# Up and down projections of a gated feed-forward block as seven block products in place of eight

## The chip, the cores and the metric

The kernel runs on one core of a Trainium2 chip. The metric is the time of one execution on the device in microseconds; a profile of one execution gives the span from its first to its last instruction. Engines are named TensorE (PE, its weight loads PEld), VectorE (DVE), ScalarE (ACT), GpSimd (POOL) and SyncE (SP, which issues DMAs).

## The reference

One layer of an encoder on 512 tokens of 2048 features, all in float32:

```python
h = rmsnorm(x, norm_mix[l])
proj = h @ w_in[l]                        # 2048 x 8704
...                                       # window attention A, neighbourhood attention B
merged = (jax.nn.sigmoid(ga) * (out_a @ w_branch_a[l])
          + jax.nn.sigmoid(gb) * (out_b @ w_branch_b[l]))
x = x + merged @ w_out[l]
h2 = rmsnorm(x, norm_ffn[l])
u = h2 @ w_up[l]                          # 2048 x 11264
u = up[:, :-2] * cw[0] + up[:, 1:-1] * cw[1] + up[:, 2:] * cw[2] + conv_b[l]   # up is u, padded
gate, val = jnp.split(u, 2, axis=-1)
x = x + (jax.nn.silu(gate) * val) @ w_down[l]   # 5632 x 2048
```

The change concerns the last five lines: the product with `w_up`, a convolution of width 3 over the tokens, the gate, and the product with `w_down`.

## The kernel before, in words

Activations lie with features on the 128 partitions and the 512 tokens along the free axis, 16 tiles for 2048 features. Every float32 operand of a product is split into two exact parts, `hi` (rounded to the type that TensorE multiplies at full rate) and `lo` (the rest), and a product is three matmuls: hi with hi, hi with lo, lo with hi (`run_step`, lines 146 to 175). All products are *steps*: 512 output columns of a weight matrix against 16, 8 or 4 activation tiles, in blocks of 1024 weight elements a partition (two activation tiles of 512 columns). A step accumulates in four of the eight PSUM banks, while the other four are being read out.

Weights come in by `stage` (line 118): SP issues one DMA of 512 KB into one of three buffers `raw`, ScalarE makes `hi` (line 135), VectorE `lo` (line 136), each in two buffers. One block is staged while the block before is multiplied: 24 matmuls of 512 columns.

The stages run in this order: the input projection with both attentions (the heads' softmax work is put into a queue and done behind the next step's matmuls; GpSimd takes small powers, line 192), gates and branches, the output projection with the residual into `x2` (line 563), and the gated block. That last part has eleven chunks of 512 features: `up(c)` makes gate and value for chunk c (two steps of eight blocks), each tile is scaled, convolved and gated by `conv` and its callers (lines 573 to 596), and the result is split into `acts`. `down(c - 1)` follows: four steps of two blocks whose sums are added to `x2` (line 610); the last chunk's results go out from there. The activations between up and down never leave SBUF.

The program is recorded in the order of the loops, and a scheduler puts each engine's instructions into an order of their own. SP's DMAs keep the order of the program among themselves.

Of the kernel before, what the change touches and what calls it, by code (L numbers as in the profile page):

```python
# [18 lines left out]
P = 128  # L19
D = 2048  # L20
S = 512
# [6 lines left out]
SMALLS = (("gffn", 16), ("gqb", 1), ("gkb", 1), ("sink", 8), ("gqa", 128), ("gka", 128),  # L28
          ("cos", 256), ("sin", 256), ("mask_a", 384), ("mask_b", 112),
          ("conv_w", 264), ("conv_b", 88))  # L30
N_SLOTS, N_P, N_TR, AHEAD = 60, 8, 4, 400
ATTENTION_RATE, RATE = 1.25, 3
READY = (2, 4, 6, 9, 12, 15, 16, 16)
# [4 lines left out]
def trunk_kernel(  # L38
# [10 lines left out]
    wst = pool("wst", 3)  # L49
# [3 lines left out]
    att_ctx = ExitStack()  # L53
# [35 lines left out]
    smalls = const.tile([P, small_in.shape[1]], F32, tag="smalls", name="smalls")  # L89
    part, at = {}, 0  # L90
    for name, width in SMALLS:
        part[name] = smalls[:, at:at + width]
        at += width
# [6 lines left out]
    def load_smalls():  # L100
        dma(smalls, small_in)
# [4 lines left out]
    steps, stream, queue = [], [], deque()  # L106

    def step(layout, w, cols, acts, evac, k0=0, nk=KD, before=None, pre=None, post=None, rate=RATE):
        """layout "f": out[col, tok], weights stationary; "t": out[tok, col], weights moving."""
        width = sum(n for _, n in cols)  # L110
        kpb = 1024 // width
        steps.append((layout, kpb, width, nk, acts, evac, before, pre, post, rate))
        for k in range(0, nk, kpb):
            stream.append((w, k0 + k, kpb, cols))

    staged = deque()

    def stage(pieces=1):
        if not stream:
            return  # L120
        w, k, kpb, cols = stream.pop(0)
        raw = wst.tile([P, 1024], F32, tag="raw", name="raw", bufs=3)
        hi = wst.tile([P, 1024], F32R, tag="hi", name="hi", bufs=2)
        lo = wst.tile([P, 1024], F32R, tag="lo", name="lo", bufs=2)
        view, at = raw.rearrange("p (a n) -> p a n", a=kpb), 0
        for c, n in cols:
            for a in range(0, kpb, kpb // pieces):
                b = a + kpb // pieces
                dma(
                    view[:, a:b, at:at + n],  # L130
                    w[(k + a) * P:(k + b) * P, c:c + n].rearrange("(a p) n -> p a n", p=P))
            at += n
        n = 1024 // pieces
        for c in range(0, 1024, n):
            nc.scalar.copy(hi[:, c:c + n], raw[:, c:c + n])  # L135
            nc.vector.tensor_tensor(  # L136
                lo[:, c:c + n], raw[:, c:c + n], hi[:, c:c + n].bitcast(F32), ALU.subtract)
        staged.append((hi.rearrange("p (a n) -> p a n", a=kpb),
                       lo.rearrange("p (a n) -> p a n", a=kpb)))
# [6 lines left out]
    def run_step(layout, kpb, width, nk, acts, evac, before, pre, post, rate):  # L146
# [4 lines left out]
        for kb in range(nk // kpb):  # L151
            if before:
                before(kb)
            hi, lo = staged.popleft()
            stage()
# [32 lines left out]
    # ---- RMSNorm over the features: the gain goes into the transposed activations, the  # L188
# [5 lines left out]
    def square_sum(name, k, src):  # L194
        """Squares summed over the 16 tiles of features."""
# [8 lines left out]
    def row_factor(name):  # L204
        """rs[tok, t], and the same along the free axis on every partition."""
# [7 lines left out]
        b = bank("tr" if "tr" in banks else "mm")  # L213
# [17 lines left out]
    def first_loads():  # L231
        load_xT(1)
        hT.append(split(xt[0], g=gmix[:, :1]))
        stage(2)
        load_xT(1)
        stage()
# [54 lines left out]
    def row_heads(cols, nh, rotate, finish, on_evac=None, then=(), **kw):  # L291
        """Heads out of 512 columns: rows normalised and transposed behind the next step."""
# [86 lines left out]
    def behind(finish=None):  # L379
        """Softmax of one head ahead of the transposes and the product with v of the last one."""  # L380
# [115 lines left out]
    post = {}  # L496

    def end_attention():
# [3 lines left out]
        post["pool"] = pool("post", 1)  # L502
# [3 lines left out]
    def extra(dt=F32):  # L506
        return post["pool"].tile([P, S], dt, tag="e", name="e", bufs=14)

    sga, sgb, merged, oa, ob = {}, {}, [None] * KD, [], []

    def gates(c0, store, base, alloc, **kw):
        def evac(m, ps):
            s = alloc()
            nc.vector.tensor_tensor(s, ps, rows["m"], ALU.mult)  # L514
            store[base + m] = s

        step("f", w_in, [(c0 + base * P, 512)], hT, evac, **kw)
# [3 lines left out]

    def evac_a(m, ps):
        s = sga[m]
        nc.scalar.activation(s, s, AF.Sigmoid)  # L524
# [165 lines left out]
```

## Time and profile before

| | us |
|---|---|
| median of 3 runs (lowest, highest) | 2634.92 (2634.89, 2636.03) |
| span of the profiled execution | 2634.1 |
| TensorE busy in it | 2623.6 |
| VectorE busy | 1258.4 |
| ScalarE busy | 840.8 |
| GpSimd busy | 34.4 |
| window of the up and down projections, 1192 to 2631 us | 1439 |

The profiled execution's own time is its span of 2634.1 us; the median of the runs is 0.8 us more. How to read the views that the prediction quotes: a group line gives source line, engine, operation, output<-inputs, shapes and count, then busy us and mean ns of one, then the idle time of the engine before it and what ended it. A line of a tile's view gives shortest/median/longest ns. A timeline line gives start and length in us, engine, line, operation, count. A line of the windows gives the stretch, its length, the busy us of PE, PEld, DVE, ACT and POOL with their counts, TensorE's granted clock, the DMA engines' busy share and GB/s. Matmuls overlap in TensorE's pipeline: what one costs is the time from its start to the next one's.

### The profile page before, as it was taken

The page shows a single profiled execution, that of the slowest core. Times are in us where ns is not written, and L with a number is a line of the kernel's source. Part 1 is how long each engine was busy: PE and PEld are TensorE (multiplying, and loading weights), DVE is VectorE, ACT ScalarE, POOL GpSimd, SP SyncE. Part 2 cuts the span into 40 slices and gives each one's busy share as a digit, 9 for nine tenths or more (in the row PEclk, how much of TensorE's full clock was granted, in tenths as well). Part 3 has the DMA queues.
Part 4 walks back from the last instruction along what each step waited for, and adds up shares of the span by engine and source line. Part 5 has one row for each costly group of instructions (what it writes and reads, how often), then busy time and mean ns, then how long its engine had stood idle before and what let it go on. Part 6 is the DMA issues. An engine that isn't in the chain of part 4 may idle for free.

```text
span 2634.1 us, 28831 instructions
## 1 busy us (share of the span) xinstructions
PE 2623.6 (100%) x11848; PEld 2182.7 (83%) x11848; DVE 1258.4 (48%) x1685; ACT 840.8 (32%) x1156; POOL 34.4 (1%) x38
## 2 busy tenths in 40 slices
PE   9999999999999999999999999999999999999999
PEld 7888888888888888888888888888888888888887
DVE  6565545542333344435453636363636363636364
ACT  5355544532222222323232323231323232323231
POOL 0100000000000000000000000000000000000000
PEclk9999999999999999999999999999999999999999
DMA  5322222333233323332323232333333333332333
GB/s 181 96 89 85 90 94 90 114 107 115 98 96 96 112 96 127 113 114 94 96 96 101 95 100 97 96 96 96 96 97 98 100 97 96 96 97 96 96 96 128
DMA packets 152115, 268.53 MB, mean 102 GB/s; under 512 B 9520, under 2 KB 35120, under 8 KB 151984
## 3 DMA queue, kind: packets, MB, share of 16 engines
q1 hardware_dynamic: 147376, 258.31, 30.7%
q10 hardware_dynamic: 4608, 8.39, 0.8%
q8 instruction: 92, 1.51, 0.2%
q14 instruction: 39, 0.32, 0.0%
HBM read 258.27 MB, written 8.39 MB: 101 GB/s over the span
## 4 chain that ended last, share of the span: by engine, by line
PE 100%; DMA 0%; DVE 0%; ACT 0%; issue 0%; SPq 0%; ACTq 0%
PE mm L74 96%; PE tr L74 2%; PE tr L430 1%; PE tr L288 0%; PE tr L337 0%; DMA s<-in_x_t 0%; PE mm L217 0%; PE tr L217 0%; PE mm L208 0%; ACT s L183 0%; DVE s L514 0%; DVE s L610 0%; PE tr L208 0%; ACT hi L135 0%; SPq L71 0%
## 5 line engine op out<-in xcount | busy, mean ns | idle before, releaser
L74 PE MATMUL mm<-s,hi 128*128 128x512 f32 x6528 | 1937.0, 389 | 0.9 <-DVE s L514 0.9
L74 PEld LDWEIGHTS mm<-s,hi 128*128 128x128 f32 x6528 | 1224.5, 188 | 253.7 <-ACT s L524 1.3
L74 PE MATMUL mm<-s,lo 128*128 128x512 f32 x3264 | 1193.7, 389 | 0.0
L136 DVE TENSOR_TENSOR lo<-raw,hi 128x1024 fp32r<-128x1024 f32 (+1 forms) x465 | 568.1, 1222 | 1161.7 <-ACT hi L135 1159.1
L135 ACT CAST hi<-raw 128x1024 fp32r<-128x1024 f32 (+1 forms) x465 | 489.1, 1052 | 1507.3 <-PE mm L74 1332.7
L74 PEld LDWEIGHTS mm<-s,lo 128*128 128x128 f32 x3264 | 612.6, 188 | 126.6
L74 PE MATMUL mm<-hi,s 128*128 128x512 f32 x896 | 285.5, 395 | 5.8 <-ACT hi L135 5.8
L74 PEld LDWEIGHTS mm<-hi,s 128*128 128x128 f32 x896 | 168.6, 189 | 39.0 <-ACT hi L135 5.8
L74 PE MATMUL mm<-lo,s 128*128 128x512 f32 x448 | 176.8, 396 | 0.0
L610 DVE TENSOR_TENSOR e<-mm,e 128x512 f32<-128x512 f32 x132 | 90.1, 689 | 23.5 <-PE mm L74 23.2
L74 PEld LDWEIGHTS mm<-lo,s 128*128 128x128 f32 x448 | 84.9, 190 | 16.5
L576 ACT ACTIVATE s<-t,smalls 128x512 f32<-128x512 f32 x88 | 71.4, 811 | 42.6 <-DVE t L575 42.6
L577 DVE SCALAR_TENSOR_TENSOR s<-t,smalls,s 128x511 f32<-128x511 f32 x88 | 65.8, 748 | 10.1 <-ACT s L576 9.7
L579 DVE SCALAR_TENSOR_TENSOR s<-t,smalls,s 128x511 f32<-128x511 f32 x88 | 65.9, 749 | 2.4
L575 DVE TENSOR_TENSOR t<-mm,row 128x512 f32<-128x512 f32 x88 | 60.4, 687 | 2.4 <-PE mm L74 2.4
L435 DVE TENSOR_TENSOR pl<-tr,ph 128x256 fp32r<-128x256 f32 (+1 forms) x64 | 30.2, 485 | 29.7 <-ACT ph L434 29.6
L589 ACT ACTIVATE t<-s 128x512 f32<-128x512 f32 x44 | 27.8, 631 | 51.0 <-DVE s L579 51.0
L409 ACT ACTIVATE p<-p,nm 128x256 f32<-128x256 f32 (+1 forms) x64 | 35.4, 555 | 23.8 <-DVE nm L402 15.9
L434 ACT CAST ph<-tr 128x256 fp32r<-128x256 f32 (+1 forms) x64 | 26.1, 421 | 47.4 <-PE tr L74 22.1
L610 DVE TENSOR_TENSOR s<-mm,s 128x512 f32<-128x512 f32 x44 | 30.4, 692 | 19.9 <-PE mm L74 19.9
L74 PE MATMUL tr<-ph,s 128*128 128x256 f32 (+1 forms) x128 | 37.7, 313 | 0.0
L180 ACT CAST s<-s 128x512 fp32r<-128x512 f32 x52 | 32.0, 619 | 17.5 <-DVE s L531 9.7
(102 smaller groups left out, 849.8 us busy)
## 6 DMA issues: line engine op xcount, KB each, us to landing
raw<-in_w_up SPq DMA_DIRECT2D x176, 512.0 KB, 3.5
raw<-in_w_in SPq DMA_DIRECT2D x103, 512.0 KB, 3.6
raw<-in_w_down SPq DMA_DIRECT2D x88, 512.0 KB, 3.6
raw<-in_w_in SPq DMA_DIRECT2D x66, 256.0 KB, 3.1
raw<-in_w_out SPq DMA_DIRECT2D x32, 512.0 KB, 3.7
raw<-in_w_branch_a SPq DMA_DIRECT2D x16, 512.0 KB, 3.6
raw<-in_w_branch_b SPq DMA_DIRECT2D x16, 512.0 KB, 3.7
s<-in_x_t SPq DMA_DIRECT2D x20, 256.0 KB, 6.1
```

What stands on the lines that cost most here:

```text
L74: nc.tensor.matmul(o, l, r, start=start, stop=stop, skip_group_check=True)
L135: nc.scalar.copy(hi[:, c:c + n], raw[:, c:c + n])
L136: nc.vector.tensor_tensor(lo[:, c:c + n], raw[:, c:c + n], hi[:, c:c + n].bitcast(F32), ALU.subtract)
L180: nc.scalar.copy(hi, src)
L409: nc.scalar.activation(pr[j][:, :n], pr[j][:, :n], AF.Exp, bias=nm[:, j:j + 1], accum_out=sm[:, j:j + 1])
L435: nc.vector.tensor_tensor(pl[:, :n], b[:, :n], ph[:, :n].bitcast(F32), ALU.subtract)
L575: nc.vector.tensor_tensor(u, ps, rows["f"], ALU.mult)
L576: nc.scalar.activation(o, u, AF.Identity, bias=cb[:, idx:idx + 1], scale=cw[:, idx, 1:2])
L577: nc.vector.scalar_tensor_tensor(o[:, 1:], u[:, :S - 1], cw[:, idx, 0:1], o[:, 1:], op0=ALU.mult, op1=ALU.add)
L579: nc.vector.scalar_tensor_tensor(o[:, :S - 1], u[:, 1:], cw[:, idx, 2:3], o[:, :S - 1], op0=ALU.mult, op1=ALU.add)
L589: nc.scalar.activation(sg, g, AF.Sigmoid)
L610: nc.vector.tensor_tensor(x2[m], ps, x2[m], ALU.add)
```

## The change

Both projections of the gated block become products of 2x2 blocks in seven multiplications (Strassen's, in Winograd's form). The blocks are: pairs of activation tiles (first and second 128 features of a pair), two halves of the output columns, and the two halves of the tokens (256 each). A *unit* (`Product`) is one pair of activation tiles and 256 columns out of each half of the output: seven weight forms of 256 columns, seven activation forms, 42 matmuls of 256 tokens.

- Weight forms: SP loads five of the seven 256-column pieces of a unit from DRAM (640 KB in three DMAs, rows of 1 KB, four units ahead). A DMA issued by GpSimd adds two further pieces onto them (three units ahead), and two additions of 256 elements on GpSimd make the remaining forms (two units ahead). ScalarE and VectorE split the forms as before, in parts of four and three forms (1024 and 768 elements), one unit ahead.
- Activation forms: `forms` makes seven forms of a pair with four subtractions or additions and seven splits of 256 elements on VectorE and seven copies on ScalarE.
- Sums: a group of units with the same columns (8 in the up projection; 8 or 7 in the down projection) accumulates seven PSUM banks; `combine` puts the four output blocks together, one ScalarE copy and seven VectorE instructions, into tiles of 1024 elements.
- The up projection runs first, 22 groups. Scaling with the row factor moves to GpSimd (line 767, 1024 elements, twice a group). The gated activations are written to DRAM (`act`, line 792) and read back in the down projection (line 835).
- The down projection runs in three parts of 8, 7 and 7 pairs. The sums of the first two parts are added by DMAs from GpSimd onto `total` in DRAM, where the residual `x2` has been put before; the last part adds them on VectorE and writes the output.
- Ahead of that, gates and branches are reordered (gate tiles are held in fewer buffers), and the staging buffers are freed after the output projection for the split weight forms.

The core of the diff:

```diff
-    def up(c):
-        ...
-        step("f", w_up, [(c * 512, 512)], h2T, evac_gate, before=before)
-        step("f", w_up, [(D_FF + c * 512, 512)], h2T, evac_val)
-    def down(c, acts, last):
-        ...
-            step("f", w_down, [(n * 512, 512)], acts, evac, k0=c * 4, nk=4)
+    def advance():
+        for phase, d in (("load", 4), ("add", 3), ("sums", 2)):
+            while at[phase] < min(at["use"] + d + 1, len(units)):
+                ...
+                    getattr(u, phase)()
+                at[phase] += 1
+        prep_to(at["use"] + 1)
+    class Product:
+        def load(self):
+            s = slice(self.c, self.c + 256)
+            self.f = ffn["f"].tile([P, 7, 256], F32, tag="f", name="f", bufs=4)
+            dma(self.f[:, 0:2], self.w[:, :, 0, s])
+            dma(self.f[:, 2:4], self.w[:, 0, :, s])
+            dma(self.f[:, 6], self.w[:, 1, 1, s])
+        def add(self):
+            tc.keep_in_program_order(nc.gpsimd.dma_start(
+                self.f[:, 2:4], self.w[:, :, 1, s], accum_op=ALU.add))
+        def sums(self):
+            nc.gpsimd.tensor_tensor(f[:, 4], f[:, 2], f[:, 6], ALU.add)
+            nc.gpsimd.tensor_tensor(f[:, 5], f[:, 4], f[:, 1], ALU.add)
+        def prep(self):
+            for tag, a, b in (("a", 0, 4), ("b", 4, 7)):
+                ...
+                nc.scalar.copy(hi, self.f[:, a:b])
+                nc.vector.tensor_tensor(lo, self.f[:, a:b], hi.bitcast(F32), ALU.subtract)
+    def forms(src):
+        nc.vector.tensor_tensor(t[:, 0], y[:, 3], y[:, 1], ALU.subtract)
+        nc.vector.tensor_tensor(t[:, 1], y[:, 0], y[:, 1], ALU.subtract)
+        nc.vector.tensor_tensor(t[:, 2], t[:, 0], y[:, 0], ALU.add)
+        nc.vector.tensor_tensor(t[:, 3], t[:, 2], y[:, 2], ALU.subtract)
+        for v in (y[:, 0], y[:, 2], t[:, 0], t[:, 1], t[:, 2], y[:, 3], t[:, 3]):
+            nc.scalar.copy(o[:, :256], v)
+            nc.vector.tensor_tensor(o[:, 256:], v, o[:, :256].bitcast(F32), ALU.subtract)
+    def products(w, c, pairs, acts, evac, before=None):
+            for i, j in enumerate(pairs):
+                u = next_unit()
+                for f, (wh, wl) in enumerate(u.parts):
+                    a = acts[j][f]
+                    for m in range(2):
+                            mm(o, wh[:, s], a[:, :256], i == m == 0, False)
+                            mm(o, wh[:, s], a[:, 256:], False, False)
+                        mm(o, wl[:, s], a[:, :256], False, i == len(pairs) - 1 and m == 1)
+                if i == len(pairs) - 1:
+                    combine(ps, evac)
+                advance()
+                run_queued(1)
+    def combine(ps, evac):
+        q1, q2, q7, q5, q6, q3, q4 = [p.rearrange("p (m n) -> p m n", m=2) for p in ps]
+        nc.scalar.copy(p1, q1)
+        nc.vector.tensor_tensor(top[:, :, left], q2, p1, ALU.add)
+        nc.vector.tensor_tensor(p1, p1, q6, ALU.subtract)
+        nc.vector.scalar_tensor_tensor(u3, q7, -1.0, p1, op0=ALU.mult, op1=ALU.subtract)
+        nc.vector.tensor_tensor(low[:, :, right], u3, q5, ALU.subtract)
+        nc.vector.tensor_tensor(p1, p1, q5, ALU.add)
+        nc.vector.tensor_tensor(top[:, :, right], q3, p1, ALU.add)
+        nc.vector.tensor_tensor(low[:, :, left], u3, q4, ALU.subtract)
+    def conv(u, idx):
+        nc.gpsimd.tensor_tensor(u, u, row, ALU.mult)
+        ...
+            def val_part():
+                v = conv(val, 44 + 2 * s)
+                nc.vector.tensor_tensor(v, gate, v, ALU.mult)
+                dma(act[s], v)
+    def down(part, pairs, nxt=()):
+                    if nxt:
+                        nc.gpsimd.dma_start(total[h][s], t, accum_op=ALU.add)
+                    else:
+                        nc.vector.tensor_tensor(t, t, old[h], ALU.add)
+                        ...
+                if s == 3 and skip <= i < skip + len(nxt):
+                    form_down(part + 1, nxt[i - skip])
+    for s in range(pairs_ff):
+        up(s)
+    down(0, range(0, 8), range(8, 15))
+    down(1, range(8, 15), range(15, 22))
+    down(2, range(15, 22))
```

The order of SP's DMAs in the middle of the up and down projections before (`raw` is a weight buffer; every row is a run of loads):

```order
L71 DMA raw<-in_w_up 128x2x512 x16
L71 DMA raw<-in_w_down 128x2x512 x8
L71 DMA raw<-in_w_up 128x2x512 x16
L71 DMA raw<-in_w_down 128x2x512 x8
L71 DMA raw<-in_w_up 128x2x512 x16
```

And SP's order around the end of one up group after (`f` are a unit's weight pieces, `act_138` the activations in DRAM, `w_14327` the tile that holds the gated values; two rows are one unit's loads, the ones behind the store are the loads of the seventh unit of the next group):

```order
L73 DMA f<-in_w_up 128x2x256 x2
L73 DMA f<-in_w_up 128x256
L73 DMA f<-in_w_up 128x2x256 x2
L73 DMA f<-in_w_up 128x256
L73 DMA act_138<-w_14327 128x1024
L73 DMA f<-in_w_up 128x2x256 x2
L73 DMA f<-in_w_up 128x256
```

A store of activations has come into the row of loads, which had nothing but loads before.

VectorE's order in an up step before (`lo` is the split of a weight block, lines 575 to 595 are the convolution and the gate):

```order
L595 TENSOR_TENSOR s<-s 128x512
L136 TENSOR_TENSOR lo<-raw,hi 128x1024
L181 TENSOR_TENSOR s<-s 128x512
L577 SCALAR_TENSOR_TENSOR s<-t,smalls,s 128x511
L579 SCALAR_TENSOR_TENSOR s<-t,smalls,s 128x511
L595 TENSOR_TENSOR s<-s 128x512
L136 TENSOR_TENSOR lo<-raw,hi 128x1024
```

VectorE's order behind the end of the same up group after (lines 631 to 635 are `combine`, line 569 the split of weight forms, `w_14226` and `w_14327` gate and value):

```order
L631 SCALAR_TENSOR_TENSOR t<-mm,t 128x512
L569 TENSOR_TENSOR wl<-f,wh 128x768
L632 TENSOR_TENSOR w_14227<-t,mm 128x2x256
L633 TENSOR_TENSOR t<-t,mm 128x512
L635 TENSOR_TENSOR w_14227<-t,mm 128x2x256
L634 TENSOR_TENSOR w_14226<-mm,t 128x2x256
```

```order
L787 TENSOR_TENSOR w_14226<-w_14226,w_14253 128x1024
L569 TENSOR_TENSOR wl<-f,wh 128x768
L569 TENSOR_TENSOR wl<-f,wh 128x1024
L791 TENSOR_TENSOR w_14327<-w_14226,w_14327 128x1024
L569 TENSOR_TENSOR wl<-f,wh 128x768
L569 TENSOR_TENSOR wl<-f,wh 128x1024
```

The splits of the weight forms now stand between the steps of `combine` and of the gate; the last product of a group (line 791), for which the store waits, stands behind the first split of the next group's sixth unit.

More of the change, by code (lines that the diff above doesn't have):

```diff
@@ L111, in step @@
         kpb = 1024 // width
-        steps.append((layout, kpb, width, nk, acts, evac, before, pre, post, rate))
+        steps.append(partial(
+            run_step, layout, kpb, width, nk, acts, evac, before, pre, post, rate))
         for k in range(0, nk, kpb):
[L114 to L139, printed above, removed]
@@ L141, in run_queued, with next_unit @@
+    def next_unit():
+        u = units[at["use"]]
+        at["use"] += 1
+        return u
     def run_queued(n):
```

296 lines of the change are left out of this document (214 added, 82 removed).

## Prediction

> **What bounds the kernel now.** I read the page's first and fourth parts, then the chain in order of time, then the busy time by windows of the span.
>
> ```profile
> span 2634.1 us, 28831 instructions
> PE 2623.6 (100%) x11848; PEld 2182.7 (83%) x11848; DVE 1258.4 (48%) x1685; ACT 840.8 (32%) x1156; POOL 34.4 (1%) x38
> PE 100%; DMA 0%; DVE 0%; ACT 0%; issue 0%; SPq 0%; ACTq 0%
> 1227.18 1403.09 PE mm L74 x6190
> 520.00:1165.00 645.00, 644.13 (x2863) 533.85 (x2862) 243.66 (x279) 183.06 (x226) 0.00 (x0) 1.00 0.34 108
> 1192.00:2631.00 1439.00, 1438.26 (x6354) 1190.83 (x6352) 705.33 (x848) 397.09 (x444) 1.93 (x1) 1.00 0.31 98
> ```
>
> TensorE is the chain from end to end, at a granted clock of 1.00. Its last piece is 6,190 matmuls of 512 columns in 1403.09 us: 226.7 ns from one to the next. The two projections of the last block (up and down) fill the window from 1192 to 2631 us: 1439 us, in which VectorE works 705 us, ScalarE 397 us, GpSimd 2 us, and the DMA engines 31% of the time at 98 GB/s. Everything but TensorE has room. So the change is worth what it takes off TensorE in these 1439 us, less what its new work makes TensorE wait.
>
> **Fewer columns.** Before: 88 x 16 x 3 matmuls for the up projection and 16 x 44 x 3 for the down, 6336 of 512 columns. After: 264 units (22 groups of 8 up, 88 units down), each with seven products x two tiles of output columns x three split terms = 42 matmuls of 256 columns: 11088. The columns fall to 7/8. The price of a 256-column matmul stands in the attention stage. These rows are TensorE's timeline at two places: start, length, what, count.
>
> ```profile
> 126.38 0.52 PE L74 MATMUL tr<-s 128*128 128x256 f32 x3
> 126.73 0.63 PE L74 MATMUL mm<-hi,s 128*128 128x512 f32 x2
> 137.34 0.52 PE L74 MATMUL tr<-s 128*128 128x256 f32 x3
> 137.70 0.40 PE L74 MATMUL mm<-lo,s 128*128 128x512 f32 x1
> L74 PEld LDWEIGHTS mm<-s,hi 128*128 128x128 f32 x6528 | 1224.5, 188 | 253.7 <-ACT s L524 1.3
> ```
>
> Three take 0.35 us and 0.36 us until the next begins: 117 to 120 ns each, 118 taken, although each has its own weight load of 188 ns. Half of 226.7 would be 113; the narrow matmul costs 4% more a column. 11088 x 0.118 = 1308 us, against 1439: **131 us off**, and 122 to 142 at 119 and 117. A unit is 42 x 0.118 = 4.96 us, a group of eight 39.65 us.
>
> **The work per unit that TensorE must not wait for.** These are groups by line and shape (count, busy us, mean ns).
>
> ```profile
> L136 DVE TENSOR_TENSOR lo<-raw,hi 128x1024 fp32r<-128x1024 f32 x463 | 566.8, 1224 | 1161.7 <-ACT hi L135 1159.1 <-PE mm L74 2.2
> L135 ACT CAST hi<-raw 128x1024 fp32r<-128x1024 f32 x463 | 487.8, 1054 | 1507.3 <-PE mm L74 1332.7 <-issue 170.9 <-DMA raw<-in_w_in 1.1
> L181 DVE TENSOR_TENSOR s<-s 128x512 fp32r<-128x512 f32 x52 | 35.6, 685 | 0.2
> L610 DVE TENSOR_TENSOR e<-mm,e 128x512 f32<-128x512 f32 x132 | 90.1, 689 | 23.5 <-PE mm L74 23.2
> L579 DVE SCALAR_TENSOR_TENSOR s<-t,smalls,s 128x511 f32<-128x511 f32 x88 | 65.9, 749 | 2.4
> L281 DVE TENSOR_TENSOR qr<-t 128x256 f32<-128x256 f32 x8 | 3.4, 420 | 0.0
> L434 ACT CAST ph<-tr 128x256 fp32r<-128x256 f32 x32 | 11.9, 371 | 40.0 <-PE tr L74 21.2 <-PE tr L430 15.6 <-DVE rq L261 3.2
> ```
>
> The seven weight forms are split as 1024 and 768 elements. VectorE: 1.22 us, and 0.96 (halfway between 685 and 1224), 2.18 us a unit. ScalarE 1.05 and about 0.84. Both fit into 4.96 us. An up group has on VectorE 8 x 2.18 for the splits, 7 x 0.69 for putting the products together, 8 x 0.75 for the convolution and 2 x 1.22 for the gate: 30.7 us of 39.65. ScalarE has about 21. Cover enough on average; the order decides.
>
> **The store in the load queue.** SP issues weight loads and activation stores in one order. In the order of the changed program, the store of a group's activation (line 792) stands ahead of the load of the seventh unit of the next group. It waits for VectorE's last product (line 791), which stands behind the first split of the sixth unit, whose buffers TensorE frees when it is done with the first four forms of the fourth unit. So load, adding DMA and split of the seventh unit begin late. The rows for it: landing times of DMAs, SP's time for one issue, and who SP waits for now.
>
> ```profile
> raw<-in_w_in SPq DMA_DIRECT2D x66, 256.0 KB, 3.1
> out_a<-o ACTq DMA_DIRECT2D x8, 256.0 KB, 2.0
> s<-in_x_t SPq DMA_DIRECT2D x20, 256.0 KB, 6.1
> L71 SPq DMA_DIRECT2D raw<-in_w_up x176: 367/368/368, 1172.6 to 2518.2; - x176
> SPq L71 <- DVE lo L136: 2255.8, 446, 9.0
> ```
>
> SP waits for buffers already (2256 us in all), but loads run far enough ahead. Now, from the start of the fourth unit: first four forms 24 x 0.118 = 2.83; ScalarE 1.05; VectorE 1.22 and 1.22; three issues on SP and the landing of 256 KB in rows of 1 KB, 3 x 0.37 + 3.1 = 4.2; the adding DMA; ScalarE 1.05. That is 11.6 us and the adding DMA. No row shows such a DMA. Its bounds are the 2.0 and 6.1 us above, and I take 3.5, nearest the 3.1 of the same bytes in the same rows: 15.1 us, where TensorE is ready after 3 x 4.96 = 14.9, and the low half comes 1.2 later on VectorE. The wait is 0 at the low bound and 4.0 at the high; I take **2 us a group, 22 x 2 = +44**. The Trainium skill (DMA: Bandwidth & Descriptors, Anatomy of one DMA) fits a GpSimd-issued DMA as 2.0 us + bytes / 436e3, here an estimate of 2.6 us; the wait would be some 1 us a group and the sum 22 us less.
>
> **Banks.** Seven of eight banks hold a group, so the next group's fifth product needs the bank that VectorE reads fifth. From the end of the old group's fifth product: the old group's last two blocks and four of the new, each 6 x 0.118 = 0.71 us, 4.25 us. VectorE needs 4 x 0.69 + 0.75 and, between them in its order, both splits of a unit, 2.18: 5.7 less the first sum, which is done early, 5.0. I take 0.5 us (0 to 1) at 34 groups: **+17**.
>
> **Activations out and back.** For the last group of the up stage and of the first two parts of the down stage, VectorE also makes the seven activation forms of each of seven pairs: 11 x 0.42 = 4.6 us a unit (ScalarE 7 x 0.37). With 2.18 that is 6.8 us against 4.96: 1.8 us late, seven times, 13 us, less if some is made in the next group's idle time. Three times 10: **+30** (0 to 39).
>
> **Ends.** At the start of the up stage the first split (1.05 + 1.22 us) waits until the last matmul of the output projection frees the memory: 5 us with what VectorE has queued for that projection. At the end four more VectorE steps and a larger store stand behind the last matmul: 5 us. **+10** (5 to 15).
>
> **At nothing.** The gates and branches are reordered, x2 goes to DRAM, and six pairs of forms are made ahead of the up stage. TensorE covers this: from 520 to 1165 us VectorE is busy 244 us of 645, and eight pairs are 37 us. Without cover it would cost those 37 us.
>
> **Sum.** 1308 + 44 + 17 + 30 + 10 = 1409 us for the window of 1439: 30 us less. The execution of 2634.1 us becomes 2604, and with the 0.8 us by which the median of the runs (2634.92) lies above the span, **2605 us**.
>
> **Rivals.**
>
> A, all waits hidden. TensorE at 117 ns, 1297 us, with 10 for the ends and half of the bank waits: 1315, so 2511 to 2540, 2520 taken. For it: VectorE has 9 us a group over, and loads run four units ahead. Against: the chain above has hardly any slack.
>
> B, GpSimd and VectorE share the reading of SBUF. The rows: GpSimd's power of 4 elements (shortest, median, longest ns), its one row that streams 128 elements, and both engines around the longest.
>
> ```profile
> L192 POOL TENSOR_TENSOR rq<-rq,mhalf x28: 697/1007/3036, 57.3 to 484.3; 128x4 f32<-128x4 f32 x24, 128x2 f32<-128x2 f32 x4
> masks.py:199 POOL TENSOR_SCALAR_AFFINE_SELECT ident<-ident 128x128 f32<-128x128 f32 x1 | 0.3, 293 | 0.0
> 105.18 4.47 POOL L192 TENSOR_TENSOR rq<-rq,mhalf 128x4 f32<-128x4 f32 x2 [4.75 <-DVE rq L191]
> 105.76 1.21 DVE L136 TENSOR_TENSOR lo<-raw,hi 128x1024 fp32r<-128x1024 f32 x1
> 106.89 0.68 DVE L278 TENSOR_TENSOR t<-qr,smalls 128x512 f32<-128x512 f32 x1
> 107.50 0.68 DVE L279 TENSOR_TENSOR t<-qr,smalls 128x512 f32<-128x512 f32 x1
> 108.10 0.68 DVE L266 TENSOR_TENSOR qr<-qr,rq 128x512 f32<-128x512 f32 x1
> ```
>
> The same GpSimd instruction takes 1007 ns and once 3036: it starts at 106.6, while VectorE runs four instructions of two SBUF operands without a gap, and ends at 109.65, 0.87 after the last (108.78). It seems to get in only when VectorE pauses. The change has GpSimd read 16 x 256 and 2 x 1024 elements a group. At 293/128 = 2.3 ns an element (an upper bound; no row has a long two-operand add there) that is 16 x 0.59 + 2 x 2.35 = 14.1 us. VectorE's instructions with two SBUF operands are 17.4 + 6.0 + 2.4 = 25.8 us. If they exclude each other they fill 39.9 of 39.65 us, and it decides from 2.24 ns an element on. If in practice GpSimd waits for all of VectorE, a group is 30.7 + 14.1 = 44.8 us: 5.2 x 22 = 114 in place of 44, **2675 us**, slower. Against: GpSimd may read while VectorE puts the products together from PSUM (4.9 us) and is idle (9 us), 13.9 us, which just holds the 14.1. The Trainium skill states this rule (SBUF — State Buffer, Who interferes with whom): a VectorE instruction with two SBUF inputs and a GpSimd instruction that reads SBUF block each other for a whole instruction. The 3036 ns above agrees. The skill's GPSIMD Engine Reference (Performance versus the Vector engine) has 4497 ns for an add of 2048 elements, by which the estimate is 2.2 ns an element, at the point of decision.
>
> C, the adding DMA lands late, in 8 us rather than 3.5, beside loads of 1 KB rows. The wait is then 22 x 6 = 132 in place of 44: **2693 us**. From 5 us on, some 3.4 us a group, the change is no gain. For it: 896 KB a unit in place of 512, 185 GB/s in place of 98. Against: loads of 1 KB rows alone reach 380 GB/s in 1.5 us slices of the attention stage.
>
> ```profile
> GB/s 85 264 0 0 0 96 380 59 0 5 35 305 10 0 0 0 89 260 0 22 307 21 0 0 29 242 265 0 0 173 176 0 0 44 301 4 0 0 117 261
> ```
>
> D, the narrow matmul is slower in a long stream than in threes, since its load is 188 ns long: at 125 ns, 1386 us, 78 more: **2683 us**. It decides from (1439 - 101) / 11088 = 120.7 ns. In that case the change doesn't take off TensorE what it says.
>
> **Chances.** The forecast, 2545 to 2629: 0.36. A: 0.18. B: 0.20. C: 0.12. D: 0.06. The waits just eat the gain, within 0.2% (5 us, about what a measurement tells from no change): 0.06. Other slower cases 0.02. So faster 0.54, same 0.06, slower 0.40. The range reaches from A's low end, 2511, to the rivals' 2695. The likeliest case's own range is 2545 to 2629.
>
> **What would show it.** In the profile after: 256-column matmuls 117 to 119 ns apart; TensorE's idle time of some 100 us in the window, in front of the seventh unit of each up group (ended by ScalarE's split) and at three changes of stage. If B holds, GpSimd's adds are far over 0.6 us and TensorE waits in all units of the up stage but few of the down stage. If C holds, the adding DMA's row shows over 5 us to landing, and ScalarE's split is ended by it. If D holds, TensorE is busy without gaps at over 120 ns. A total above 2640 or a wait in TensorE at another place proves the sum wrong.

## The result, and the profile after

The changed kernel takes 3034.34 us (median of 4 runs, 3029.97 to 3045.18), the kernel before 2635.46 (2634.89 to 2636.03): 1.152 times as long, 95% interval 1.150 to 1.154. The forecast was 2605. The page of the changed kernel, and its busy time by windows:

```profile
span 3028.1 us, 42864 instructions
PE 2653.7 (88%) x16600; PEld 2406.7 (79%) x16600; DVE 1709.2 (56%) x2157; ACT 1107.8 (37%) x1606; POOL 1031.2 (34%) x890
PE mm L76 54%; DMA f<-in_w_up 8%; DMA f<-in_w_down 6%; DVE wl L569 5%; DVE w L775 2%; PE tr L76 2%; POOL f L560 2%; ACT wh L568 2%; SPq L73 2%; POOL f L555 1%; DVE w L787 1%; POOL f L561 1%; DVE w L791 1%; DVE w L772 1%; PE tr L470 1%
```

```profile
900.00:1165.00 265.00, 264.94 (x1136) 212.87 (x1135) 117.63 (x156) 81.56 (x109) 0.00 (x0) 1.00 0.38 123
1275.00:2406.00 1131.00, 909.03 (x7060) 893.89 (x7059) 750.58 (x729) 408.55 (x487) 668.91 (x540) 0.90 0.62 148
2482.00:3018.00 536.00, 438.24 (x3362) 430.47 (x3361) 296.76 (x396) 182.59 (x267) 261.87 (x250) 0.89 0.73 175
```

TensorE was the whole chain that ended last. Now the matmuls of line 76 are 54% of it, but that counts the stages ahead too, where they are nearly all of it. From 1223 to 3018 us alone they are 30%, and loads, VectorE and GpSimd hold most of the rest:

```profile
by line: PE mm L76 29.7%; DMA f<-in_w_up 14.2%; issue 13.0%; DMA f<-in_w_down 10.2%; DVE wl L569 8.9%; DVE w L775 3.5%; POOL f L560 2.8%; ACT wh L568 2.7%; SPq L73 2.4%; POOL f L555 2.0%; DVE w L787 1.8%; POOL f L561 1.6%; DVE w L791 1.4%; 
```

GpSimd has gone from 34 to 1031 us. The granted clock has gone from 1.00 to 0.90 in the up window. No engine is full.

TensorE's long wait of an up group stands in front of the seventh unit, as the prediction said, in all groups but the first, but for 9.3 us on the mean in place of 2. Shorter waits stand ahead of the fourth and fifth units. The chain in order of time through one long wait (start, length, what; short pieces left out):

```profile
1774.43 1.61 DVE wl L569
1776.13 1.19 DVE w L775
1777.33 1.67 DVE w L787
1779.79 1.21 DVE wl L569
1781.00 1.15 DVE w L791
1782.20 0.33 SPq L73
1783.07 3.96 DMA f<-in_w_up
1787.58 7.78 DMA f<-in_w_up
1795.52 1.05 ACT wh L568
1796.61 15.42 PE mm L76 x109
```

VectorE's last product (L791), the store that SP holds until then, the load behind it (3.96 us), the adding DMA (7.78 us from GpSimd's issue), ScalarE's split, TensorE. TensorE's own timeline at that place:

```profile
1784.22 0.28 PE L76 MATMUL mm<-s,wl 128*128 128x256 f32 x1
1784.34 0.40 PE L76 MATMUL mm<-s,wh 128*128 128x256 f32 x2
1784.59 0.28 PE L76 MATMUL mm<-s,wl 128*128 128x256 f32 x1
1796.61 2.08 PE L76 MATMUL mm<-s,wh 128*128 128x256 f32 x8 [9.59 <-ACT wh L568]
1799.13 0.63 PE L76 MATMUL mm<-s,wl 128*128 128x256 f32 x2
1799.56 0.63 PE L76 MATMUL mm<-s,wh 128*128 128x256 f32 x2
```

The first three rows stand some 2 us ahead of the wait: a matmul takes 0.12 us (three in 0.37). Behind it one takes 0.215 (two in 0.43). In the up groups 9 to 28 matmuls go at this pace before the pitch is 0.12 again. The granted clock (the value behind the GpSimd time) is halved from 1791.2 to 1801.3 us:

```profile
1791.20:1801.30 10.10, 4.69 (x22) 4.69 (x23) 4.71 (x4) 3.66 (x4) 5.90 (x7) 0.50 0.73 139
```

The wait is paid twice: in idle time and in matmuls at half speed.

In the down stage GpSimd stops itself. Its timeline over one unit, and the waits of the whole trace (total, times, longest):

```profile
2533.42 1.20 POOL L555 DMA_DIRECT2D f<-in_w_down  x1
2537.84 0.73 POOL L560 TENSOR_TENSOR f<-f 128x256 f32<-128x256 f32 x1 [3.23 <-DMA f<-in_w_down]
2538.66 0.74 POOL L561 TENSOR_TENSOR f<-f 128x256 f32<-128x256 f32 x1
2539.34 1.20 POOL L555 DMA_DIRECT2D f<-in_w_down  x1
```

```profile
SPq L73 <- DVE w L791: 521.3, 22, 26.9
ACT wh L568 <- DMA f<-in_w_up: 409.1, 77, 18.0
POOL f L560 <- DMA f<-in_w_down: 241.1, 72, 6.6
```

Issue of the adding DMA, its landing, two sums, the next issue: 5.92 us from one issue to the next, where TensorE needs 5.04 a unit. In the program's order the sums of a unit stand behind the adding DMA of the *next* unit; the scheduler put 36 of the 88 sums of the down stage right behind their own. Then the groups of the new work, and the time to landing (from the start of the issue) of the plain loads and of the adding DMA:

```profile
L569 DVE TENSOR_TENSOR wl<-f,wh 128x1024 fp32r<-128x1024 f32 x264 | 413.8, 1568 | 499.9 <-ACT wh L568 494.4 <-DMA f<-in_w_down 5.0 <-DMA f<-in_w_up 0.3
L560 POOL TENSOR_TENSOR f<-f 128x256 f32<-128x256 f32 x264 | 301.1, 1141 | 447.7 <-DMA f<-in_w_down 241.1 <-DMA f<-in_w_up 205.1
L561 POOL TENSOR_TENSOR f<-f 128x256 f32<-128x256 f32 x264 | 263.9, 1000 | 20.1
L767 POOL TENSOR_TENSOR w<-w,row 128x1024 f32<-128x1024 f32 x44 | 122.9, 2815 | 1.3 <-DVE w L635 1.3
```

```profile
f<-in_w_up SPq DMA_DIRECT2D x352, 256.0 KB, 4.5
f<-in_w_up POOLq DMA_DIRECT2D x176, 256.0 KB, 5.8
```

The stage from its first to its last matmul (1223.4 to 3018.4 us) is 1795 us, against 1409 forecast. From the starts of its 11088 matmuls:

| us | forecast | measured |
|---|---|---|
| matmuls at full speed | 1308 (118 ns) | 1331 (120.0 ns) |
| in front of the seventh unit of 22 groups | 44 | 196 |
| other waits in up groups (banks in the forecast) | 17 | 51 |
| three changes of stage | 30 | 61 |
| other waits in down groups | 0 | 78 |
| 817 matmuls at about 215 ns | 0 | 77 |
| ends (behind the last matmul) | 5 of 10 | 6 more than before |

The measured rows but the last sum to 1794. The stage also begins 31 us later, at 1223 in place of 1192, though TensorE hardly rests ahead of it.

### The profile page after: what moved, and what is told of

The parts are those of the page before. It is cut to its first block, busy times and chain, and to the rows that moved or that the text cites. A ratio compares the mean times of both kernels' runs of the same rounds, so it can differ in the third digit from the quotient of the medians.

```text
span 3028.1 us, 42864 instructions
## 1 busy us (share of the span) xinstructions
PE 2653.7 (88%) x16600; PEld 2406.7 (79%) x16600; DVE 1709.2 (56%) x2157; ACT 1107.8 (37%) x1606; POOL 1031.2 (34%) x890
## 4 chain that ended last, share of the span: by engine, by line
PE 57%; DMA 15%; DVE 12%; issue 8%; POOL 4%; ACT 2%; SPq 2%; DVEq 0%; ACTq 0%; POOLq 0%
PE mm L76 54%; DMA f<-in_w_up 8%; DMA f<-in_w_down 6%; DVE wl L569 5%; DVE w L775 2%; PE tr L76 2%; POOL f L560 2%; ACT wh L568 2%; SPq L73 2%; POOL f L555 1%; DVE w L787 1%; POOL f L561 1%; DVE w L791 1%; DVE w L772 1%; PE tr L470 1%
## 5 line engine op out<-in xcount | busy, mean ns | idle before, releaser
L76 PE MATMUL mm<-s,wh 128*128 128x256 f32 x7392 | 1388.2, 293 | 310.7 <-ACT wh L568 285.2
L76 PEld LDWEIGHTS mm<-s,wh 128*128 128x128 f32 x7392 | 1186.4, 199 | 320.6 <-ACT wh L568 293.6
L76 PE MATMUL mm<-s,wl 128*128 128x256 f32 x3696 | 1038.6, 292 | 40.2 <-DVE wl L569 40.0
L569 DVE TENSOR_TENSOR wl<-f,wh 128x1024 fp32r<-128x1024 f32 (+1 forms) x528 | 701.1, 1349 | 607.8 <-ACT wh L568 598.7
L568 ACT CAST wh<-f 128x1024 fp32r<-128x1024 f32 (+1 forms) x528 | 489.8, 941 | 1016.3 <-DMA f<-in_w_up 409.1
L76 PEld LDWEIGHTS mm<-s,wl 128*128 128x128 f32 x3696 | 710.6, 197 | 55.0 <-DVE wl L569 54.6
L76 PE MATMUL mm<-s,hi 128*128 128x512 f32 x2304 | 703.4, 396 | 2.1 <-ACT s L221 2.0
L76 PEld LDWEIGHTS mm<-s,hi 128*128 128x128 f32 x2304 | 431.7, 188 | 105.3 <-ACT s L221 2.5
L560 POOL TENSOR_TENSOR f<-f 128x256 f32<-128x256 f32 x264 | 301.1, 1141 | 447.7 <-DMA f<-in_w_down 241.1
L76 PE MATMUL mm<-s,lo 128*128 128x512 f32 x1152 | 429.3, 395 | 0.0
L561 POOL TENSOR_TENSOR f<-f 128x256 f32<-128x256 f32 x264 | 263.9, 1000 | 20.1
```

What stands on the lines that cost most here:

```text
L76: nc.tensor.matmul(o, l, r, start=start, stop=stop, skip_group_check=True)
L560: nc.gpsimd.tensor_tensor(f[:, 4], f[:, 2], f[:, 6], ALU.add)
L561: nc.gpsimd.tensor_tensor(f[:, 5], f[:, 4], f[:, 1], ALU.add)
L568: nc.scalar.copy(hi, self.f[:, a:b])
L569: nc.vector.tensor_tensor(lo, self.f[:, a:b], hi.bitcast(F32), ALU.subtract)
```

## The experiments

Up groups are 336 matmuls; their length in a run is read from the count in the window from 1400 to 2000 us. Single runs, each beside a run of the kernel before at 2634.9 to 2636.0 us. TensorE alone would need 40.3 us a group (336 x 0.12); the changed kernel needs 53.7:

```profile
1400.00:2000.00 600.00, 482.23 (x3754) 474.00 (x3753) 397.43 (x370) 212.38 (x245) 355.67 (x288) 0.91 0.61 146
```

**The store later.**

```diff
-                dma(act[s], v)
             queue.extend((gate_part, val_part))
+            if s < pairs_ff - 2:
+                queue.extend([lambda: None] * 3 + [lambda: dma(act[s], held["v"])])
```

> One edit of the changed kernel: the store of a group's activations is recorded four units later, so that SP gets it behind the loads of four more units (all groups but the last two). Theory S (the store in the load queue holds back the loads of the seventh unit): the waits of some 9.5 us in front of the seventh unit of an up group go in 20 of 22 groups, and with each the 1 to 3 us of matmuls at half speed behind it, some 11.5 us a group, 230 us: about 2800 us. Rival A (the adding DMA, 5.8 us to landing, is the limit by itself): the waits move to other units and 2950 us or more remain. Rival B (GpSimd and VectorE slow each other): about half of the waits stays, spread over all units, some 2900 us. GpSimd's order changes with this edit: 42 of 176 sums of the up stage now stand right behind their own unit's adding DMA (2 before), which speaks for a part of A.

2951.16 us, 83 less than the median of the changed kernel. The wait in front of the seventh unit is gone in all groups but the last, in front of which the store stays where it was, but a group still takes 49.3 us: first the window, then the waits from 1318 to 2210.

```profile
1400.00:2000.00 600.00, 530.36 (x4087) 513.51 (x4086) 402.46 (x401) 232.62 (x266) 374.43 (x315) 0.96 0.68 160
```

```profile
POOL f L560 <- DMA f<-in_w_up: 325.3, 126, 6.7
```

GpSimd sits out landings for 325 us. Theory S is a part. The time is rival A's, but that the landing alone is the limit is not shown by it, and the run without the sums below speaks against it.

**The sums behind the next adding DMA.**

```diff
-            nc.gpsimd.tensor_tensor(f[:, 4], f[:, 2], f[:, 6], ALU.add)
+            tc.keep_in_program_order(
+                nc.gpsimd.tensor_tensor(f[:, 4], f[:, 2], f[:, 6], ALU.add))
```

> One edit of the changed kernel: the first sum of each unit on GpSimd keeps its place in the order of the program, behind the adding DMA of the next unit; before, 36 of 88 sums of the down stage stood right behind their own unit's adding DMA and waited out its landing. Theory P (in the down stage GpSimd's chain of issue, landing and sums, 5.9 us a unit, is longer than TensorE's 5.0): the down stage, 612 us from 2406 to 3018, falls by 60 to 100 us, 2930 to 2970 us in all; the up stage, where only 2 of 176 stand so, stays. Rival (the adding of the sums onto DRAM, which stands in GpSimd's queue too, or the reading of the activations is what stops the down stage): less than 20 us, 3010 us.

2961.73 us. The down stage falls from 612 to 571 us, less than expected, and the up stage from 1183 to 1154. The edit is worth 73 us. It asks for another order on GpSimd alone, but by the traces the scheduler moved splits on VectorE and ScalarE as well, so how much is GpSimd's queue is not shown apart.

**Both.**

> Both edits together: the store of the activations four units later, and GpSimd's sums held behind the adding DMA of the next unit (0 of 264 sums stand right behind their own adding DMA, where the late store alone had 42 in the up stage). Theory (what is left of the waits after the late store is GpSimd sitting out the landing of its own adding DMA): an up group falls from 49.3 to 42 or 43 us, the down stage stays at the 571 us of the run with the sums in order: about 2750 us. Rival B (GpSimd and VectorE slow each other, whatever the order): groups stay at 47 us or more, about 2860 us.

2798.36 us: 236 less than the changed kernel, more than the 83 and 73 together. Groups take 44.4 us, between the two theories.

```profile
1400.00:2000.00 600.00, 564.93 (x4540) 560.85 (x4538) 502.44 (x448) 257.59 (x296) 411.60 (x350) 0.97 0.75 177
```

**No adding DMA**, the store as it was, and then late.

```diff
-            tc.keep_in_program_order(nc.gpsimd.dma_start(
-                self.f[:, 2:4], self.w[:, :, 1, s], accum_op=ALU.add))
+            pass
```

> One edit of the changed kernel: the adding DMA is left out, so that the two pieces which it adds are missing from the weight forms; everything else stays, the store in the load queue too. Theory A (the adding DMA lands late): the wait in front of the seventh unit falls from 9.5 us by the 7.9 us that issue and landing of the adding DMA took in the group from 1755 us, to 1 to 2 us, and in the down stage, where a unit took 5.9 us of GpSimd's chain (adding DMA, landing, two sums), the waits go as well: 3028 less 22 x (8 + 2) less 100 is about 2710 us. Theory S alone (the store is what holds the loads back, the adding DMA is hidden behind it): the waits in front of the seventh unit stay above 5 us, 2850 us or more.

2724.88 us, groups of 44.3. With the store still in the load queue some 2.4 us a group are left in front of the seventh unit. That this is near the forecast's 2 is chance: without the adding DMA the forecast's chain is 11.6 us against 14.9, and leaves no wait. So the adding DMA was not the only length that was too short.

> The adding DMA is left out (two pieces are missing from the weight forms), and the store of the activations is four units later. Theory (the store in the load queue costs what is left in front of the seventh unit, 2 us of waiting and 1.5 us of slow matmuls a group): an up group falls from 44.2 to about 41 us, 2725 less 70 is about 2655 us. Rival (without the adding DMA the store no longer costs anything, the rest is GpSimd beside VectorE): 2725 us stays.

2652.08 us, groups of 40.5: TensorE hardly waits in the up groups. The two windows:

```profile
1400.00:2000.00 600.00, 569.36 (x4548) 562.92 (x4547) 478.60 (x450) 257.57 (x299) 342.02 (x242) 0.97 0.40 127
```

```profile
1400.00:2000.00 600.00, 598.92 (x4975) 597.41 (x4974) 509.41 (x488) 284.82 (x329) 400.69 (x267) 1.00 0.48 144
```

**The adding DMA without the sums.** `sums` is emptied, and the second part of the split takes pieces 1 to 3 again.

> Late store; the adding DMA stays, but the two sums on GpSimd are left out (forms five to seven are copies of two to four, so the products are not those of the computation). GpSimd keeps the adding DMAs and the row factors. Against the run with both edits (2798 us, up groups of 44.4 us): theory B (GpSimd's sums and VectorE's splits slow each other and hold the group): the 1024-element split falls from 1.58 to under 1.3 us and an up group to 40.5 to 41.5 us, 2700 us. Rival A (the landing of the adding DMA holds the group whatever GpSimd does): splits get faster, groups stay at 44 us, 2790 us.

2666.54 us, groups of 40.3: in the up groups the adding DMA alone costs nothing either (the down stage takes 530 us, 513 in the run before). The 1024-element split is at 1.37 us, not under 1.3, and in the run before it was at 1.47 with no wait; so faster splits are not the reason. Nor is the traffic: 198 GB/s is the most of all runs in this window.

```profile
1400.00:2000.00 600.00, 600.00 (x5003) 600.00 (x5002) 469.23 (x495) 285.86 (x328) 224.73 (x149) 1.00 0.82 198
```

**Four pieces, no adding DMA, the whole computation.** Each distinct piece is loaded once, and one addition of 512 elements makes what the DMA added. The store is late, and the loads run three units ahead into three buffers, in place of four.

```diff
-            dma(self.f[:, 2:4], self.w[:, 0, :, s])
+            dma(self.f[:, 7], self.w[:, 0, 1, s])
+            nc.gpsimd.tensor_tensor(
+                f[:, 2:4], f[:, 0:7:6], f[:, 7:8].to_broadcast([P, 2, 256]), ALU.add)
```

> A version of the same computation without the adding DMA: SP loads the four distinct pieces of a unit once (512 KB in place of 640 and 256 KB) into three buffers, GpSimd adds 512 and 256 elements and VectorE 256 for the sums; the store of the activations is four units later. Theory (the adding DMA is what the change loses by): up groups of 42 to 44 us, a down stage of about 510 us, 2680 us. Rival B (GpSimd and VectorE shut each other out: 8 x 3.3 + 6.2 = 33 us of GpSimd and 39 us of VectorE a group): groups of 46 us or more, 2770 us or more.

2881.26 us, as rival B said and not the theory; VectorE is busy 519.8 of 600 us and TensorE waits for its splits.

> As the version with four pieces, but all three sums on GpSimd (512, 256 and 256 elements), none on VectorE, which was busy without a break there. Theory (that version was held by VectorE, 35 us plus the sums of a group of 40): GpSimd has 8 x 3.75 + 5.8 = 36 us a group and VectorE 35, up groups of 41 to 44 us, the down stage 510 us, 2680 to 2720 us. Rival B (beside VectorE GpSimd's sums grow until GpSimd is the bound): groups of 46 us or more and 2800 us or more.

2838.07 us and groups of 46.7, again as rival B said; GpSimd is busy 515 of 600 us. The 512-element sum takes 2.02 us, the split 1.60. What the shorter lead of the loads costs here was not tried apart.

```profile
1400.00:2000.00 600.00, 545.18 (x4315) 542.29 (x4313) 498.45 (x418) 244.15 (x282) 515.29 (x337) 0.94 0.34 102
```

**Where the weights lie.** Matmuls of 512 columns take 233.3 ns in the changed kernel, in stages whose products the change leaves as they were: from the chain in order of time, 529.21 us for 2268 there, and 226.7 in the kernel before, 600.21 for 2648.

```profile
599.98 529.21 PE mm L76 x2268
```

```profile
599.96 600.21 PE mm L74 x2648
```

Four edits move tiles, by an unused tile or the side of a pool, and nothing in the order of the work.

> One edit of the changed kernel: an unused tile of 32 bytes a partition ahead of the weight tiles, which moves all of them (raw, hi, lo, and the split forms) from addresses of 96 modulo 128 to 64 modulo 128, where they were in the kernel before. Theory: the address is why a 512-column matmul takes 233.5 ns in the changed kernel and 226.7 in the kernel before, in stages that the change leaves alone. Then it is 226.7 again, the up stage begins 29 to 31 us earlier (at about 1193), and the narrow matmul falls from 119.7 to about 117 ns (28 us more, if the groups don't wait for something else): 2970 to 3000 us. Rival (the longer program, or the clock): 233.5 and 119.7 ns stay, 3028 us.

232.4 ns, 3031.99 us: not the theory's 226.7.

> The kernel before with one edit: the pool of the weight tiles lies at the top of the memory, as in the changed kernel (hi at 212960 and 217056 bytes, before at 38720 and 42816); the order of the instructions is the same on every engine. Theory (where the weights lie relative to the activations sets the time of a matmul): the 512-column matmul goes from 226.7 to about 233.4 ns, and the time up by some 75 us, 2710 us. Rival (the length or the kind of the changed program does it): 226.7 ns and 2635 us stay.

2706.83 us, 233.3 ns: the place alone makes the kernel before 71 us slower.

> The kernel before with one edit: 1152 unused bytes between the weight tiles and the activation tiles; the weights stay low (hi at 38720), the activations move from 55104 to 56256 and up, which is the distance modulo 2048 that the changed kernel with moved weights had (where a 512-column matmul took 232.4 ns). Theory H1 (the height of the weights' address sets the time of the matmul): 226.7 ns and 2635 us stay. Theory H2 (the distance of weights and activations modulo some power of two does): about 232 ns and 2690 us.

2702.09 us, 232.4 ns, with the weights as low as before: the height is not what counts.

> The changed kernel with one edit: the sides of the memory are exchanged, so that the weight tiles lie low (hi at 33600) and the activations, weight pieces and wide tiles high; the order on every engine is unchanged. Theory H1 (height of the weights): 226.7 ns for the 512-column matmul and about 117 for the narrow one, the up stage begins some 30 us earlier, at 1193, and the time is 2970 to 3000 us. Theory H2 (distance modulo a power of two) has no forecast of its own, 226.7 to 233.4 ns.

232.4 ns, 3031.84 us; the distance was 128 bytes modulo 512 here, as in the two runs with 232.4 above.

```diff
+    pad = pool("pad", 1, side="right").tile([P, 40], F32, tag="pad", name="pad")
+    nc.gpsimd.memset(pad, 0.0)
```

> The changed kernel with one edit: 160 unused bytes at the top of the memory, so that the weight tiles (hi at 212800) lie a multiple of 512 bytes from the activations (21312), as they do in the kernel before; the distance was 160 bytes modulo 512. Theory (the distance modulo 512 sets the time of a matmul): 226.7 ns for 512 columns, about 117 for 256; the up stage begins at about 1193, and with 2.5 ns on 11088 narrow matmuls the time is 2970 us. Rival (only the distance modulo 2048 counts, or the height): 232 ns and 3028 us stay.

226.7 ns again (475.32 us for 2097), and the up stage begins at 1198. But the narrow matmul stays at 120.0 ns, and the stage itself takes 1805 us in place of 1795: 3015.01 us. In the three runs at 128 bytes the narrow matmul took 118.8 to 119.1 ns, less than at 0, though the wide one took more: the two sizes don't follow one rule.

```profile
599.86 475.32 PE mm L78 x2097
```

In both layouts with 226.7 ns the weights and the activations each lie 320 bytes above a multiple of 512 (38720 and 55104, 212800 and 21312), and in all others one of the two doesn't. So the runs don't tell the distance from each tile's own place, nor 512 from 256 or 1024.

**What can be reached.** First with the adding left out, then complete, then with one piece of work less for GpSimd.

> Late store, adding DMA left out (two pieces are missing from the weight forms), weights 512 bytes apart from the activations. It shows what the scheme could reach if the adding were free. Theory (distance modulo 512): 2652 us less 31 ahead of the up stage less 11088 x 2.5 ns is 2593 us, faster than the kernel before. Rival: the distance does nothing, 2652 us.

2617.91 us, 0.7% under the kernel before, with two pieces of the weight forms missing: the stage takes 1409.5 us from its first to its last matmul. 64 us of waits, most of them at the changes of stage, and 14 us of slow matmuls are left.

> The complete computation with the three edits that each helped: late store, GpSimd's sums behind the next adding DMA, weights 512 bytes apart from the activations. Theory: 2798 less 31 ahead of the up stage less some 25 us for the narrow matmuls: 2740 us, still slower than the kernel before. If the waits for GpSimd eat the shorter matmuls: 2767 us.

2770.13 us, groups of 44.2.

```diff
-        nc.gpsimd.tensor_tensor(u, u, row, ALU.mult)
+        nc.vector.tensor_tensor(u, u, row, ALU.mult)
```

> The best complete version so far (late store, sums behind the next adding DMA, weights 512 bytes apart; 2770 us, up groups of 44.5 us) with one edit: the scaling by the row factor, 2 x 2.9 us a group on GpSimd, goes to VectorE (2 x 1.22). Theory G (the waits that are left come from GpSimd's own queue, in which an adding DMA or a sum stands behind 5.8 us of scaling): up groups of 41 to 42 us, 2770 less 22 x 3 is about 2705 us. Rival V (VectorE, 36.5 us of 44.5 busy, becomes the bound): groups stay at 44 us or grow, 2770 us or more. Rival A (landing time of the adding DMA): 44 us stay.

2721.71 us, groups of 42.0: theory G. GpSimd was less than 70% busy in this window in either run, first with the scaling on GpSimd, then on VectorE:

```profile
1400.00:2000.00 600.00, 568.99 (x4561) 565.13 (x4562) 491.28 (x448) 258.15 (x297) 415.93 (x353) 0.97 0.75 181
```

```profile
1400.00:2000.00 600.00, 584.40 (x4804) 579.26 (x4802) 518.46 (x496) 271.20 (x315) 393.41 (x346) 1.00 0.80 190
```

> All edits together: four pieces with the sums on GpSimd, the late store, the weights low, and the putting together of a group's products ahead of other work on VectorE. Theory: the time of the version with four pieces on GpSimd (2680 to 2720), less 30 us ahead of the up stage, less up to 30 us for narrow matmuls of 117 in place of 119.7 ns, less some 10 us at each of three changes of stage: 2600 to 2640 us, at or just under the kernel before. If the place of the weights does nothing here: 2650 us or more.

2837.7 us, as without its two extra edits: the weights lay 128 bytes modulo 512 away, and GpSimd was busy 512 of 600 us. No complete version is faster than the kernel before; the best stands at 2721.71, 3.3% over it.

## Why the prediction was wrong, point by point

- **The failed step** is the term of the store in the load queue, +44, which measured 196. Place, chain and the unit that waits were right; two lengths of the chain were not. From the start of the fourth unit (1770.1) to TensorE's next matmul it took 26.5 us in place of 15.1: to the end of L791 12.1 in place of 6.3, load 4.9 in place of 4.2, adding DMA with issue 8.3 in place of 3.5, split 1.2. TensorE was through with the sixth unit after some 16.8 us. (By the forecast's own rows the wait is 1.4 us, and 2 were taken.) With one of the two as forecast and the other as measured, an estimate from these numbers still leaves a wait of 4 to 5 us.
- **VectorE's way to L791** was counted as one split and L791 itself, "VectorE 1.22 and 1.22". From 1774.43 to 1782.15 VectorE ran six instructions in 7.7 us (the rows above show five): three splits, a convolution (L775) and both products of the gate (L787, L791). Where a sum or scaling of GpSimd stood beside them they were slower: over the whole trace a 1024-element split takes 1.21 us with none beside it and 1.86 with one beside more than half of it.
- **The adding DMA**: "No row shows such a DMA ... I take 3.5". Its median is 5.8 us to landing, of which 1.26 is GpSimd's issue. In this chain it took 7.8 from the start of the issue, 7.3 on the mean of 21 groups, more than the upper bound of 6.1, a plain load's landing.
- **The term that was missing** is GpSimd's queue. "Everything but TensorE has room" was read from busy shares. GpSimd issues the adding DMA, and behind it in the same order stand sums that wait for a landing, and two scalings of 2.8 us a group. Leaving out the adding DMA takes 299 us off the version with the late store, leaving out the sums 285: in the up groups either alone costs nothing, and the two together nearly 9 us a group. Both runs also shorten the path from load to split, and so don't tell this path from the queue. Holding the sums behind the next adding DMA and moving the scaling away leave all work to be done, and gave 153 us and 48 us on top of other edits; they speak for the queue.
- **Fewer columns** was nearly right: 120.0 ns in place of 118, +23 us, and 118.8 to 120.0 over the runs, just under rival D's 120.7.
- **Banks** (+17): no wait of that kind in the up groups. **Activations** (+30): 61 at the changes of stage, of which 25 end with VectorE's read of a bank (L629, four waits), so the two terms can't be told apart there. **Ends** (+10): 12, of which 6 at the start (1198 with the weights in place, 1192 before) and 6 at the end.
- **At nothing**: wrong by 25 us (1223.4 less 1198.1), and not for lack of cover. The weights' pool went to the other end of the memory, 160 bytes off a multiple of 512 from the activations, and each wide matmul took 6.6 ns more.
- **The clock** had no term: 817 matmuls at about 215 ns, 77 us, at a granted clock of 0.50 in the window above. The Trainium skill (TensorE: Matmul & The Clock Gate, Part 1) states that an idle window of about 3.4 us halves TensorE's clock, and a busy one restores it. The rows agree on the half, 0.12 and 0.215 us, but not on the length: in the run with both edits nine single waits of 2.4 to 2.6 us were each followed by 17 or 18 slow matmuls.
- **Rivals.** C was nearest in its sign: the adding DMA lands late, and ScalarE's split is ended by it. It gave 2693, since it too counted one wait a group, in the up stage, at full clock; and late landing alone is not the cause, since without the sums it costs an up group nothing. B's slowing is there (sums of 1.14 us on the mean; 0.73 with VectorE idle, 1.44 with VectorE busy throughout), but with the adding DMA left out the same slowing costs no wait; where GpSimd or VectorE gets more work (four pieces), it may decide. A and D fell.
- **Shown and argued.** Shown by taking away or moving: the store, adding DMA and sums, the scaling, the place of the tiles. That the order of GpSimd's queue is what the held sums gain by is argued. The half speed is read from the rows, with no experiment of its own. What the last 1.7 us of an up group are made of, and how to mend the changes of stage (some 60 us), stays open.

The +44 accounts for 152 of some 390 us that the stage took more than forecast; 78 are other waits in down groups, 77 the slow matmuls, the rest smaller terms. With the adding free and the weights in place the stage took 1409.5 us, and the forecast was 1409; but the terms differ, and the sum agrees by luck.

## What to carry to other kernels

Price an engine that gets new work by its queue, not by its busy share: write down what stands behind each of its waits, above all when it issues a DMA whose landing it then waits for. In the changed kernel's trace every wait of TensorE of 3 us or more was followed by 1.0 to 2.9 us lost in slow matmuls, so a term for idle time needs a second one. When pools move, compare addresses of weights and activations before and after, since the place alone was worth 71 us of 2635 here.

## What the runs showed of the hardware

- Distance of weights and activations modulo 512 bytes, and the time of a 512-column matmul: 0: 226.7 ns (before, and the changed kernel with 160 unused bytes); 128: 232.4 (three layouts); 160: 233.3 (two). The 256-column matmul took 120.0 ns at 0 and at 160, and 118.8 to 119.1 at 128.
- An adding DMA of 256 KB: 1.26 us of GpSimd for the issue, 5.8 us to landing where plain loads of the same size took 4.5 (both from the start of the issue).
- A GpSimd sum of 256 elements: 0.73 us beside an idle VectorE, 1.0 to 1.6 us in the means of these runs.
- 256-column matmuls of 0.215 us in place of 0.12 where the granted clock is 0.50: behind the waits of 8 to 11 us in front of the seventh unit, and behind single waits of TensorE as short as 2.4 us (the run with both edits).
